# Two rows in place of one: where layer two of an encoder keeps the two parts of its activations

## The chip, the cores and the metric

The kernel runs on one core of a Trainium2 chip. The metric is the device time of one launch in microseconds. It was 2395.79 us, the median of three runs (2395.14 to 2395.84). The profile page and the trace come from one further execution, which took 2398.91 us.

## The reference

Two layers of a bidirectional encoder trunk over 16 learned meta tokens and 256 grid tokens (272 positions, model width 2048). Cut to what matters here:

```python
def _layer(h, w_in, ...):
    proj = einsum('bld,dp->blp', h, w_in)            # 2048 -> 6176 columns
    y_gla = _gla_mixer(gq, gk, gv, gr, glr, ...)     # gated linear attention, 4 heads
    y_na = _na_mixer(nq, nk, nv, na_rel_bias)        # 2-D neighbourhood attention, 16 heads
    mix = einsum('blm,md->bld', concatenate([y_gla, y_na]), w_out)   # 2048 -> 2048
    h = _layer_norm(DEEPNORM_ALPHA * h + mix, ln1_w, ln1_b)
    ff = einsum('blf,fd->bld', square(relu(einsum('bld,df->blf', h, w_ff1))), w_ff2)
    return _layer_norm(DEEPNORM_ALPHA * h + ff, ln2_w, ln2_b)        # 2048 -> 8192 -> 2048
```

The meta tokens are dropped from the output, so the second layer computes many of its products for the 256 grid tokens alone.

## The kernel before

**Activations** lie transposed: a chunk is 128 of the 2048 features on the partitions, positions along the free dimension. There are 16 chunks of `x` (the residual stream, 272 or 256 positions), 16 of `y` (the mixer outputs, later the first half of an MLP hidden half) and 16 of `u` (the other part of the MLP hidden half). Each chunk is kept as two parts, a rounded high part and the remainder, the low part. Both lie in one tile of `ROOM` = 640 floats. Method `pair` opens the tile and `parts` places the two parts in it: the high one `home` floats in, the low one `apart` floats behind the high one. The table `WIDE` gives `(home, apart)`. Layer one uses the first entry. In layer two `x` uses the second while it holds more than 256 columns, and the third, `(36, T)` with T = 256, is used for `y`, `u` and for `x` once the MLP has its normed values: there the two parts touch and make one row of 512 floats.

**Weights** are streamed from memory in tiles of 128 x 1024 floats (512 KB). `made` (from line 138 on) issues the load on the SP queue, ScalarE writes the high part `wh` (line 152) and VectorE the low part `wl` (line 153). Three buffers of each are in rotation. `STARTS` fixes where `wh` and `wl` begin in their buffers for each layer; all of layer two uses the same starts.

**Products.** An exact-enough product is the sum of three: high weight by high part, high weight by low part, low weight by high part. `by_m` walks the output blocks of 128 rows, and for each block the 16 (or, in the second MLP product, 32) input chunks; `three` issues the matmuls of one chunk. With 272, 274 or 258 columns these are three matmuls (lines 165, 166, 167). With exactly 256 columns they are two, here called a pair:

```python
        if n == T:
            mm(ps, lhsT=wh[:, c:c + P], rhs=x.joined, start=first, stop=False)
            mm(ps[:, T:], lhsT=wl[:, c:c + P], rhs=xh[:, :T], start=False, stop=last)
            return
```

The first (line 161) streams both parts, 512 columns, against one load of the high weights; the second (line 162) streams the high part against the low weights. `joined` is an access pattern over both parts: 512 floats in a row where they touch, and two rows of 256 otherwise. `by_k` (line 191) is a second order, used where the input chunks become ready one after another: it takes two chunks at a time for four output blocks and reads the parts separately.

**Order of layer two.** Projections (K, V, q, the output gates, then q, k and v of the neighbourhood attention), in which work of the two attentions is put between the chunks by `pump`; the output projection (first four output blocks by `by_k`, the other twelve by `by_m`); the MLP in two halves, each with eight groups of four output blocks of the first product (inputs `x`) and then 16 blocks of the second product (inputs `y` and `u`). In the first half, groups 0 and 1 use the values before the norm with 258 columns (`fixed`), group 2 is a `by_k` that brings in the normed values through `normed` and `renew`, and all others are pairs. `renew` writes the normed chunk over the old one; in the MLP of layer two it first moves the parts to the third entry of `WIDE`.

Of the kernel before, what the change touches and what calls it, by code (L numbers as in the profile page):

```python
# [17 lines left out]
T = 256  # L18
# [18 lines left out]


ROOM = 640
WIDE = (23, 276), (3, 288), (36, T)  # L40
STARTS = (40, 48), (0, 8)


# [8 lines left out]
class Trunk:  # L52
# [88 lines left out]
    def made(self, ap, parts, l):  # L141
        if ap is None:
            return None
        nc = self.nc
        size = ap.shape[-1]
        raw = self.wp.tile([P, WB], F32, name="raw", tag="raw")[:, :size]
        wh, wl = (self.wp.tile([P, WB + 64], F32R, name=nm, tag=nm)[:, at:at + size]
                  for nm, at in zip(("wh", "wl"), STARTS[l]))
        for p in range(parts):
            c = slice(p * size // parts, (p + 1) * size // parts)  # L150
            nc.sync.dma_start(raw[:, c], ap[:, c])
            nc.scalar.copy(wh[:, c], raw[:, c])  # L152
            self.wl = nc.vector.tensor_tensor(wl[:, c], raw[:, c], wh[:, c].bitcast(F32), ALU.subtract).ins  # L153
        return wh, wl
# [67 lines left out]
    def pair(self, pool, name, c, late=None):  # L222
        if name == "sp":
            return Pair(pool.tile([P, 2, L], F32R, name=f"{name}{c}", tag=f"{name}{c}", bufs=1))
        t = pool.tile([P, ROOM], F32R, name=f"{name}{c}", tag=f"{name}{c}", bufs=1)
        return self.parts(t, *WIDE[(2 if name != "x" else 1) if (self.l if late is None else late) else 0])

    def parts(self, t, home, apart):

        both = t[:, home:home + 2 * apart].rearrange("p (a c) -> p a c", a=2)  # L230
        made = Pair(both)
        made.tile, made.joined = t, t[:, home:home + 2 * T] if apart == T else both[:, :, :T]
        return made


# [635 lines left out]
    def renew(self, end):  # L871

        f = self.norm
        n = f["n"]
        for c in range(f["new"], end):
            while f["ready"] <= c:
                self.step(self.bg, 1)
            if n == T:
                self.x[c] = self.parts(self.x[c].tile, *WIDE[2])
            h, lo = self.x[c]  # L880
            self.split(self.acc[:, c, :n], h[:, :n], lo[:, :n])
        f["new"] = end
# [138 lines left out]
```

## Time and profile before

| | |
|---|---|
| median of three runs | 2395.79 us |
| the profiled execution | 2398.91 us, of which the span is 2396.5 us |
| granted TensorE clock | 0.997 |
| busy: TensorE / VectorE / ScalarE / GpSimd | 2363.8 / 1575.8 / 1187.7 / 284.4 us |
| matmuls | 17276 |
| matmuls of line 161 (512 columns) on x, y, u | 1152, 704, 512 |
| matmuls of line 162 (256 columns) on x, y, u | 1152, 704, 512 |
| read from HBM | 412.57 MB |

Layer two begins at about 1212 us with its K projection. Its projections end at about 1558 us, the output projection at 1652, the MLP's last matmul starts at about 2378 us, and the final norm and the output follow.

How to read it: "busy" of TensorE counts the union of the matmuls' durations, and matmuls overlap, so the pace of a stream is read from the starts in the timeline and not from the busy time. A matmul of 512 columns that takes some 390 to 400 ns starts only some 230 ns ahead of the next.

### The profile page before, as it was taken

The numbers are of one execution on the slowest core, as the hardware profiler recorded it, in microseconds if no ns is written. First come the engines' busy times: TensorE is split into PE (matmuls) and PEld (weight loads), VectorE is DVE, ScalarE is ACT, GpSimd is POOL, SyncE is SP. The second block draws the span as 40 slices with busy tenths as digits, with TensorE's granted clock in tenths as the row PEclk, the third lists the DMA queues.
The fourth block names the chain that finished last, engine by engine and source line by source line (L and its number), as shares of the span: only waits on it lengthen the run. The fifth ranks groups of instructions, "written<-read, shape, count | busy, mean of one in ns | idle before, by whom it ended". The sixth has DMA issues, their size and how long they took to land.

```text
span 2396.5 us, 43078 instructions
## 1 busy us (share of the span) xinstructions
PE 2363.8 (99%) x17276; PEld 2239.3 (93%) x17276; DVE 1575.8 (66%) x2473; ACT 1187.7 (50%) x1962; POOL 284.4 (12%) x447
## 2 busy tenths in 40 slices
PE   9999999999999999999999999999999999999997
PEld 9999999999999999999999898989988888888886
DVE  6688777775544455556577987778765545665655
ACT  6555555564433344444456656555644334444443
POOL 1164320010000000000020653201100000000000
PEclk9999999999999999999999999999999999999998
DMA  7544444555555555555555454455565655565553
GB/s 247 167 142 148 139 147 159 177 182 178 179 182 178 182 177 181 180 178 181 179 178 180 141 153 151 148 166 185 185 188 188 187 185 185 187 188 186 185 188 129
DMA packets 118359, 417.46 MB, mean 174 GB/s; under 512 B 13388, under 2 KB 16332, under 8 KB 118160
## 3 DMA queue, kind: packets, MB, share of 16 engines
q1 hardware_dynamic: 118160, 414.72, 54.6%
q8 instruction: 135, 2.21, 0.4%
q14 instruction: 64, 0.52, 0.1%
HBM read 412.57 MB, written 2.10 MB: 173 GB/s over the span
## 4 chain that ended last, share of the span: by engine, by line
PE 91%; DVE 4%; POOL 2%; issue 1%; ACT 1%; DMA 0%; SPq 0%; ACTq 0%; POOLq 0%; DVEq 0%
PE mm L161 22%; PE mm L165 16%; PE mm L166 16%; PE mm L167 16%; PE mm L162 11%; PE mm L191 5%; POOL lev L475 1%; PE bg L505 1%; DVE wl L153 1%; PE bg L648 1%; DVE acc L864 1%; PE bg L597 0%; ACT ns L580 0%; ACT wh L152 0%; DVE lev L481 0%
## 5 line engine op out<-in xcount | busy, mean ns | idle before, releaser
L153 DVE TENSOR_TENSOR wl<-raw,wh 128x1024 fp32r<-128x1024 f32 (+1 forms) x772 | 945.7, 1226 | 639.1 <-ACT wh L152 630.8
L152 ACT CAST wh<-raw 128x1024 fp32r<-128x1024 f32 (+1 forms) x772 | 804.6, 1043 | 928.2 <-PE mm L166 334.0
L165 PE MATMUL mm<-x,wh 128*128 128x272 f32 (+2 forms) x2176 | 624.3, 287 | 0.0
L166 PE MATMUL mm<-x,wh 128*128 128x272 f32 (+2 forms) x2176 | 617.9, 284 | 0.0
L167 PE MATMUL mm<-x,wl 128*128 128x272 f32 (+2 forms) x2176 | 617.2, 284 | 0.1
L166 PEld LDWEIGHTS mm<-x,wh 128*128 128x128 f32 x2176 | 409.3, 188 | 0.0
L161 PE MATMUL mm<-x,wh 128*128 128x512 f32 x1152 | 409.0, 399 | 0.0
L165 PEld LDWEIGHTS mm<-x,wh 128*128 128x128 f32 x2176 | 407.9, 187 | 1.2 <-issue 0.4
L167 PEld LDWEIGHTS mm<-x,wl 128*128 128x128 f32 x2176 | 407.9, 187 | 0.5 <-DVE wl L153 0.3
L162 PE MATMUL mm<-x,wl 128*128 128x256 f32 x1152 | 323.0, 280 | 0.2 <-DVE wl L153 0.2
L161 PEld LDWEIGHTS mm<-x,wh 128*128 128x128 f32 x1152 | 216.2, 188 | 49.8 <-issue 0.4
L161 PE MATMUL mm<-y,wh 128*128 128x512 f32 x704 | 249.4, 397 | 0.0
L162 PEld LDWEIGHTS mm<-x,wl 128*128 128x128 f32 x1152 | 220.6, 191 | 0.7 <-DVE wl L153 0.6
L166 PE MATMUL mm<-y,wh 128*128 128x272 f32 x704 | 199.2, 283 | 0.0
L165 PE MATMUL mm<-y,wh 128*128 128x272 f32 x704 | 199.2, 283 | 0.0
L167 PE MATMUL mm<-y,wl 128*128 128x272 f32 x704 | 198.9, 283 | 0.0
L162 PE MATMUL mm<-y,wl 128*128 128x256 f32 x704 | 197.2, 281 | 0.7 <-DVE wl L153 0.7
L161 PE MATMUL mm<-u,wh 128*128 128x512 f32 x512 | 181.7, 397 | 0.0
L475 POOL TENSOR_TENSOR lev<-be 128x128 f32<-128x128 f32 (+1 forms) x256 | 150.2, 617 | 112.3 <-PE bg L505 36.3
L161 PEld LDWEIGHTS mm<-y,wh 128*128 128x128 f32 x704 | 132.0, 188 | 30.6 <-ACT wh L152 0.2
L165 PE MATMUL mm<-u,wh 128*128 128x272 f32 x512 | 144.9, 283 | 0.0
L166 PE MATMUL mm<-u,wh 128*128 128x272 f32 x512 | 144.9, 283 | 0.0
(235 smaller groups left out, 3319.4 us busy)
## 6 DMA issues: line engine op xcount, KB each, us to landing
raw<-in_wff SPq DMA_DIRECT2D x512, 512.0 KB, 3.5
raw<-in_win SPq DMA_DIRECT2D x190, 512.0 KB, 3.6
raw<-in_wout SPq DMA_DIRECT2D x64, 512.0 KB, 3.6
nb<-in_nab SPq DMA_DIRECT2D x16, 352.0 KB, 3.9
out<-acc SPq DMA_DIRECT2D x8, 256.0 KB, 2.2
xraw<-in_xT SPq DMA_DIRECT2D x7, 272.0 KB, 5.3
wraw<-in_wup SPq DMA_DIRECT2D x2, 392.0 KB
raw<-in_win SPq DMA_DIRECT2D x4, 128.0 KB, 2.7
```

The lines of the kernel that those rows point to most:

```text
L152: nc.scalar.copy(wh[:, c], raw[:, c])
L153: self.wl = nc.vector.tensor_tensor(wl[:, c], raw[:, c], wh[:, c].bitcast(F32), ALU.subtract).ins
L161: mm(ps, lhsT=wh[:, c:c + P], rhs=x.joined, start=first, stop=False)
L162: mm(ps[:, T:], lhsT=wl[:, c:c + P], rhs=xh[:, :T], start=False, stop=last)
L165: mm(o, lhsT=wh[:, c:c + P], rhs=xh[:, :n], start=first, stop=False)
L166: mm(o, lhsT=wh[:, c:c + P], rhs=xl[:, :n], start=False, stop=False)
L167: mm(o, lhsT=wl[:, c:c + P], rhs=xh[:, :n], start=False, stop=last)
L191: self.nc.tensor.matmul(ps[m][:, :n], lhsT=parts[p][0][:, c:c + P], rhs=acts[j][parts[p][1]][:, :n], start=j + p == 0, stop=j == nk - 1 an ...
L475: tt = lambda o, x, y: nc.gpsimd.tensor_tensor(o, x, y, ALU.subtract)
L505: nc.tensor.matmul(ps[:, b], lhsT=k[:, b], rhs=q[:, r], start=True, stop=True)
L648: nc.tensor.matmul(r[hs], lhsT=(v2 if rest else v1)[:, t, hs], rhs=p2[:, t, :] if rest else p1[:, 2 * t + hh, :], start=rest, stop=not rest)
L864: return self.nc.vector.tensor_tensor(v, v, by[:, None, :].to_broadcast([P, m, n]), alu)
```

## The change

The third entry of `WIDE` goes. Every chunk of layer two, `y` and `u` included, takes the second entry: the high part 3 floats into the tile and the low part 288 floats behind it. `x` stays where it is when `renew` writes the normed values. `joined` is then always the two-row pattern over both parts. The numbers 76 and 204 modulo 256 are the byte addresses of the two rows. No instruction is added or taken away.

```diff
-WIDE = (23, 276), (3, 288), (36, T)
+WIDE = (23, 276), (3, 288)
...
         t = pool.tile([P, ROOM], F32R, name=f"{name}{c}", tag=f"{name}{c}", bufs=1)
-        return self.parts(t, *WIDE[(2 if name != "x" else 1) if (self.l if late is None else late) else 0])
+        return self.parts(t, *WIDE[1 if (self.l if late is None else late) else 0])
 
     def parts(self, t, home, apart):
         both = t[:, home:home + 2 * apart].rearrange("p (a c) -> p a c", a=2)
         made = Pair(both)
-        made.tile, made.joined = t, t[:, home:home + 2 * T] if apart == T else both[:, :, :T]
+        made.joined = both[:, :, :T]
         return made
...
             while f["ready"] <= c:
                 self.step(self.bg, 1)
-            if n == T:
-                self.x[c] = self.parts(self.x[c].tile, *WIDE[2])
             h, lo = self.x[c]
             self.split(self.acc[:, c, :n], h[:, :n], lo[:, :n])
```

## The prediction

> **What bounds the kernel now.** I read the page first: the shares of the engines and the chain that ended last.
>
> ```profile
> span 2396.5 us, 43078 instructions
> PE 2363.8 (99%) x17276; PEld 2239.3 (93%) x17276; DVE 1575.8 (66%) x2473; ACT 1187.7 (50%) x1962; POOL 284.4 (12%) x447
> PE 91%; DVE 4%; POOL 2%; issue 1%; ACT 1%; DMA 0%; SPq 0%; ACTq 0%; POOLq 0%; DVEq 0%
> ```
>
> TensorE is busy for 99% and carries 91% of the chain, so time moves only if TensorE's stream moves. A busy TensorE says nothing of its pace, so next I cut the end of layer two into stretches (columns: length, then busy time and count by engine, granted clock, DMA share, GB/s).
>
> ```profile
> 2016.00:2197.00 181.00, 181.00 (x1026) 158.20 (x1025) 113.16 (x159) 84.98 (x126) 0.00 (x0) 1.00 0.59 186
> 2248.00:2378.00 130.00, 130.00 (x743) 113.15 (x742) 77.87 (x109) 52.75 (x62) 0.00 (x0) 1.00 0.53 170
> 2378.00:2396.50 18.50, 1.15 (x5) 0.59 (x4) 13.24 (x23) 8.32 (x17) 5.70 (x3) 0.58 0.33 113
> ```
>
> In the MLP (the first two rows, TensorE's busy time second) TensorE has no idle time at the full granted clock. What follows its last product is 18.5 us of final norm and output, which the change leaves alone. Whatever the MLP gains comes off the end one for one.
>
> **The pace of a pair.** Where a chunk has 256 columns, line 161 streams high and low part together (512 columns) and line 162 the high part (256): one pair per 128 input rows. Layer two has pairs in both layouts already. The projections read x as two rows (home 3, 288 apart: 12 and 1164 bytes into the tile). The output projection and the MLP read one row (home 36: 144 bytes in). If 12 is 76 modulo 256, a tile starts at 64, the second row lies at 204, and the one row starts at 208. Tiles are 640 floats, ten times 256 bytes, so all of one pool share that residue. The groups by form for four stretches: the q projection, the output projection, a part of that, and the MLP on both sides of 2248 us (count | busy time, mean ns of one | idle before):
>
> ```profile
> L161 PE MATMUL mm<-x,wh 128*128 128x512 f32 x64 | 22.5, 391 | 0.0
> L162 PE MATMUL mm<-x,wl 128*128 128x256 f32 x63 | 17.5, 277 | 0.0
> L161 PE MATMUL mm<-y,wh 128*128 128x512 f32 x192 | 67.5, 397 | 0.0
> L161 PE MATMUL mm<-y,wh 128*128 128x512 f32 x24 | 8.2, 389 | 0.0
> L161 PE MATMUL mm<-x,wh 128*128 128x512 f32 x832 | 294.1, 399 | 0.0
> L162 PE MATMUL mm<-x,wl 128*128 128x256 f32 x832 | 233.8, 281 | 0.0
> L161 PE MATMUL mm<-y,wh 128*128 128x512 f32 x336 | 119.7, 399 | 0.0
> L161 PE MATMUL mm<-u,wh 128*128 128x512 f32 x320 | 114.0, 399 | 0.0
> L161 PE MATMUL mm<-u,wh 128*128 128x512 f32 x192 | 67.7, 395 | 0.0
> L161 PE MATMUL mm<-y,wh 128*128 128x512 f32 x177 | 62.7, 395 | 0.0
> ```
>
> Two rows: 391 and 277 ns (first pair of lines). One row: 397 in the output projection, with a part of it at 389; in the MLP 399 and 281 until about 2248 us, then 395. Products overlap, so the pace has to come from starts. The timeline of TensorE gives the first and last start of unbroken stretches:
>
> ```profile
> 1263.83 0.39 PE L161 MATMUL mm<-x,wh 128*128 128x512 f32 x1
> ...
> 1271.11 0.39 PE L161 MATMUL mm<-x,wh 128*128 128x512 f32 x1
> ...
> 1538.50 0.39 PE L161 MATMUL mm<-x,wh 128*128 128x512 f32 x1
> ...
> 1542.66 0.39 PE L161 MATMUL mm<-x,wh 128*128 128x512 f32 x1
> ...
> 1589.11 0.28 PE L772 MATMUL bg<-sp,onesr 128*128 128x256 f32 x1
> ...
> 1589.68 0.39 PE L161 MATMUL mm<-y,wh 128*128 128x512 f32 x1
> ...
> 1597.16 0.39 PE L161 MATMUL mm<-y,wh 128*128 128x512 f32 x1
> ...
> 1722.14 0.39 PE L161 MATMUL mm<-x,wh 128*128 128x512 f32 x1
> 1722.37 0.28 PE L162 MATMUL mm<-x,wl 128*128 128x256 f32 x1
> 1722.48 0.40 PE L161 MATMUL mm<-x,wh 128*128 128x512 f32 x1
> 1722.72 0.28 PE L162 MATMUL mm<-x,wl 128*128 128x256 f32 x1
> 1722.84 0.40 PE L161 MATMUL mm<-x,wh 128*128 128x512 f32 x1
> ...
> 2016.10 0.40 PE L161 MATMUL mm<-x,wh 128*128 128x512 f32 x1
> ...
> 2197.01 0.40 PE L161 MATMUL mm<-y,wh 128*128 128x512 f32 x1
> ...
> 2248.07 0.28 PE L772 MATMUL bg<-sp,onesr 128*128 128x256 f32 x1
> ...
> 2250.05 0.40 PE L161 MATMUL mm<-u,wh 128*128 128x512 f32 x1
> ...
> 2332.30 0.39 PE L161 MATMUL mm<-y,wh 128*128 128x512 f32 x1
> ```
>
> - Two rows, q projection: 21 pairs in 7.28 us, 346.7 ns a pair.
> - Two rows, last projection: 12 pairs in 4.16 us, 346.7 ns.
> - One row, MLP: 512 pairs in 180.91 us (32 output blocks of 16 chunks), 353.3 ns.
> - One row, after about 2250 us: 235 pairs in 82.25 us, 350.0 ns.
> - One row, a stretch of the output projection: 22 pairs in 7.48 us, 340.0 ns.
>
> So one layout holds three paces at one clock. The stretch at 350.0 begins just after a foreign matmul (the mean of a norm, line 772, at 2248.07) breaks the stream, and so does the one at 340.0 (1589.11): a stream of pairs settles into a rhythm that depends on how it was last broken. The two-row stream is broken every 8 to 24 pairs by attention work, and both stretches quoted, 270 us apart, come back to 346.7.
>
> **The change, part by part.**
>
> 1. *The joined read of line 161 and the 256-column read of line 162.* Pairs affected: output projection 12 products x 16 chunks = 192; the MLP up to the break 832 + 336 + 320 = 1488; after it 192 + 176 = 368 (one of the 177 straddles the cut). Together 2048. I take 346.7 for all of them, since it is the same instruction form with the same weight offsets at the same residues.
>    MLP up to the break: 1488 x (353.3 - 346.7) = 9.8 us. After it: 368 x (350.0 - 346.7) = 1.2 us. The output projection mixes paces: its mean of 397 ns lies a fifth of the way from 399 (pace 353.3) to 389 (pace 340.0), so I estimate 353.3 - 0.2 x 13.3 = 350.6, and 192 x 3.9 = 0.7 us. Sum 11.7 us.
>    Bounds: the best and worst pace that a pair shows here, 340.0 and 353.3. At 340.0: 1488 x 13.3 + 368 x 10.0 + 192 x 10.6 = 19.8 + 3.7 + 2.0 = 25.5 us. At 353.3 everywhere: 368 x 3.3 + 192 x 2.7 = 1.7 us lost. I stay at 346.7, the row nearest in form and place.
>
> 2. *The 384 products of line 191* (third MLP group, and the first of the output projection) read high and low part separately, now at 76 and 204 in place of two places both 208 modulo 256.
>
> ```profile
> 1262.76 0.29 PE L191 MATMUL mm<-x,wh 128*128 128x272 f32 x1
> ...
> 1263.13 0.39 PE L161 MATMUL mm<-x,wh 128*128 128x512 f32 x1
> ...
> 1652.13 0.29 PE L165 MATMUL mm<-x,wh 128*128 128x258 f32 x1
> ...
> 1657.98 0.51 PE L772 MATMUL bg<-sp,onesr 128*128 128x256 f32 x3
> ...
> 1699.49 0.28 PE L191 MATMUL mm<-x,wh 128*128 128x256 f32 x1
> ```
>
>    Now they take (1722.14 - 1699.49) / 192 = 118.0 ns. At the new residues the nearest rows are the last three 272-column products of the group that reads x before the q projection, (1263.13 - 1262.76) / 3 = 123 ns, and the 48 products of 258 columns, (1657.98 - 1652.13) / 48 = 121.9 ns. 256 columns cost 0.24 - 0.12 = 0.12 us by the steps after 1722.48, 0.47 ns a column, so these scale to some 116 and 121 for 256 columns: 384 x (-2 to +3) = -0.8 to +1.2 us. I take 0, as the same line lies on the gaining side and the other on the losing side.
>
> 3. *What writes the chunks* (the split on ScalarE and VectorE at lines 213 and 214) writes the same counts of 256 columns, only elsewhere: no instruction is added or removed. Their cover is the busy TensorE; ScalarE has 96 of 181 us free in the first row of the stretches and VectorE 68.
>
> 4. *The move of x inside its tile* when the normed values replace the raw ones goes away. Its new row overlapped both old ones; now each part lands on its own predecessor. The matmuls waiting on it show no idle time at 1699.49, so 0 either way.
>
> 5. *The weight stream.* A faster TensorE asks for each 512 KB tile every 8 x 346.7 = 2.774 us in place of 2.826. No DMA moves in the program, but this is what would be late next.
>
> ```profile
> SPq L151 <- DVE wl L153: 191.5, 79, 3.7
> q1 hardware_dynamic: 26661, 97.06, 58.8%
> ```
>
>    In the MLP the queue itself waits for VectorE to free a raw buffer (191.5 us in 79 waits) with the rings 58.8% filled, and VectorE in turn is paced by what TensorE has read. At 340.0 (2.72 us a tile) nothing starved for 22 pairs. So nothing.
>
> Sum: 11.7 us. The profiled execution took 2398.91 us (span 2396.5 and 2.4 around it), 3.1 above the median 2395.79; the pairs are the same in both, so I take the saving off the median: 2384.1 us, 0.5% faster.
>
> **The rivals.**
>
> *No change.* The rhythm belongs to the stage and not to the layout: two rows look faster only because attention breaks the stream, and in a stream unbroken for 100 us they too settle at 353.3. Time: 2395.8 + 1.7 at most, some 2396.5. For it: one layout shows three paces. Against: the one row reaches its slow rhythm within a pair or two of 1722.14 (starts 1722.14, 1722.48 and then 353 apart), while two rows hold 346.7 over 21 pairs.
>
> *The good rhythm.* Two rows settle at 340.0 in the MLP. Time 2395.8 - 25.5 = 2370.3. For it: such a rhythm exists. Against: only with one row, and for some 24 pairs of 192.
>
> *Slower: the rows start off a line.* Both 76 and 204 are 12 past a multiple of 16 where 208 is a multiple, so a joined read touches 130 pieces of 16 bytes in place of 128 and line 162 65 in place of 64. If each piece more costs the four columns that it holds, 4 x 0.47 = 1.9 ns, a pair takes 5.6 ns more: 2048 x 5.6 = +11.5 us, 2407.3. It decides if the joined read in the MLP keeps its 399 ns and pays this on top. For it: the 258-column products read 76 and 204 in a long stream at 121.9 ns, above the 118.0 of the reads at 208. Against: the projections' joined read pays no such price, 391 ns against 399.
> The Trainium skill has this rule in "SBUF — State Buffer", Specifications: SBUF lines are 16 bytes and each crossing to a new one pays a penalty. By that rule alone the change could only lose; this trace's 391 against 399 disagrees.
>
> **How the numbers follow.** A measurement of this kernel tells 0.2%, 4.8 us, from no change. Pace 346.7 or near it in nearly all of the stream: 0.76, 2382 to 2387. A mixture of 346.7 with stretches at 350 and above: 0.06, 2387 to 2392. The good rhythm: 0.05, 2370. No change: 0.07. Slower: 0.06. Faster is 0.76 + 0.05 + 0.05 of the mixtures (those under 2391.0) = 0.86; same 0.07 + 0.01 = 0.08; slower 0.06. The range takes in the likeliest case, its unknown of -0.8 to +1.2 us, the mixtures, and half of the way to the good rhythm: 2377 to 2392, leaving out some 0.18.
>
> **What the profile after would show.** Right: line 161 with x, y and u in the MLP at 391 ns and line 162 at 277; 512 pairs of the second half's first product in 177.5 us in place of 180.9; the busy TensorE shorter by 12 us; the queue still waiting for VectorE. Step 2 right: line 191 at 280 to 282 ns. Wrong: 399 in the MLP (the stage sets the rhythm), or 391 with waits of line 161 or 162 on VectorE or ScalarE at the weights (the stream of weights is next), or a pace above 353.

## The result, and the profile after

The kernel after took 2386.38 us (median, 2386.06 to 2386.67) against 2395.67 for the kernel before, six runs each: a ratio of 0.9961, 95% interval 0.9948 to 0.9974. Timed again in a later round it took 2386.69 us, at 0.9949 (0.9936 to 0.9961) of the kernel before. It was forecast at 2384.1; the gain was 9.3 us where 11.7 were forecast.

The page of the kernel after: span, busy times, and the chain that ended last.

```profile
span 2384.2 us, 43078 instructions
PE 2351.7 (99%) x17276; PEld 2230.9 (94%) x17276; DVE 1576.1 (66%) x2473; ACT 1187.5 (50%) x1962; POOL 283.5 (12%) x447
PE 92%; DVE 4%; POOL 2%; issue 1%; ACT 1%; DMA 0%; SPq 0%; ACTq 0%; POOLq 0%; DVEq 0%
```

The instructions are the same in number, TensorE is 12.1 us less busy with its matmuls (PE) and 8.4 us less with its weight loads (PEld), and the span is 12.3 us shorter; no other engine moved by a microsecond. The groups by form of the kernel after (count | busy time, mean ns of one | idle before): the output projection, the MLP up to the foreign matmul near its end, and the rest.

```profile
L161 PE MATMUL mm<-y,wh 128*128 128x512 f32 x192 | 66.6, 391 | 0.0
...
L161 PE MATMUL mm<-x,wh 128*128 128x512 f32 x832 | 288.5, 391 | 0.0
L162 PE MATMUL mm<-x,wl 128*128 128x256 f32 x832 | 231.0, 278 | 0.0
L161 PE MATMUL mm<-y,wh 128*128 128x512 f32 x336 | 117.5, 391 | 0.0
...
L161 PE MATMUL mm<-u,wh 128*128 128x512 f32 x192 | 67.1, 390 | 0.0
L161 PE MATMUL mm<-y,wh 128*128 128x512 f32 x176 | 61.7, 390 | 0.0
```

The 399 ns are gone everywhere. The line of the 832 pairs on x holds the pace too: each product of line 161 outlasts the step to the next pair, so the busy time of an unbroken group is its stretch, and 288.5 / 832 = 346.8 ns (before, 294.1 / 832 = 353.5). This is 0.1 to 0.2 ns above the step from starts, as the last product of each stretch counts in full. Most experiments below are read by this line. The timeline of TensorE shows the pace directly, and the borders of the stages:

```profile
1583.28 0.39 PE L161 MATMUL mm<-y,wh 128*128 128x512 f32 x1
...
1651.20 0.28 PE L165 MATMUL mm<-x,wh 128*128 128x258 f32 x1
...
1698.50 0.28 PE L191 MATMUL mm<-x,wh 128*128 128x256 f32 x1
...
1720.87 0.39 PE L161 MATMUL mm<-x,wh 128*128 128x512 f32 x1
...
2009.30 0.39 PE L161 MATMUL mm<-x,wh 128*128 128x512 f32 x1
...
2186.79 0.39 PE L161 MATMUL mm<-y,wh 128*128 128x512 f32 x1
...
2236.92 0.28 PE L772 MATMUL bg<-sp,onesr 128*128 128x256 f32 x1
...
2237.51 0.39 PE L161 MATMUL mm<-u,wh 128*128 128x512 f32 x1
...
2320.36 0.39 PE L161 MATMUL mm<-y,wh 128*128 128x512 f32 x1
...
2365.17 0.39 PE L161 MATMUL mm<-u,wh 128*128 128x512 f32 x1
```

512 pairs of the second half's first product take 177.49 us, 346.7 ns each. Over all 2048 pairs, line 162 starts 230 ns behind line 161 where it was 237, and the next pair 117 ns behind line 162 where it was 116: the gain lies behind the 512-column product. After the foreign matmul of 2236.92, where the kernel before had changed to 350.0, 239 pairs take 82.85 us, 346.7 ns again. Two more rows of the kernel before, its first and last pair of the stages in question, complete the comparison:

```profile
1583.28 0.39 PE L161 MATMUL mm<-y,wh 128*128 128x512 f32 x1
...
2377.49 0.40 PE L161 MATMUL mm<-u,wh 128*128 128x512 f32 x1
```

Output projection, pairs: 68.85 to 67.92 us, 0.9 gained. MLP, first to last pair: 655.35 to 644.30, 11.05 gained. Third MLP group (line 191): 22.65 to 22.37, 0.3 gained. That is the whole of the 12.3 us between the profiles but for 0.05.

The SP queue's own waits up to the foreign matmul, and the stretch that answers to the first one shown of before:

```profile
SPq L151 <- DVE wl L153: 187.4, 79, 3.7
2009.00:2187.00 178.00, 178.00 (x1028) 155.92 (x1028) 113.17 (x159) 85.07 (x127) 0.00 (x0) 1.00 0.61 190
```

The queue still waits for VectorE, and TensorE never for weights.

### The profile page after: what moved, and what is told of

Read it like the earlier page. It is cut to its first block, busy times and chain, and to the rows that moved or that the text cites. A ratio compares the mean times of both kernels' runs of the same rounds, so it can differ in the third digit from the quotient of the medians.

```text
span 2384.2 us, 43078 instructions
## 1 busy us (share of the span) xinstructions
PE 2351.7 (99%) x17276; PEld 2230.9 (94%) x17276; DVE 1576.1 (66%) x2473; ACT 1187.5 (50%) x1962; POOL 283.5 (12%) x447
## 4 chain that ended last, share of the span: by engine, by line
PE 92%; DVE 4%; POOL 2%; issue 1%; ACT 1%; DMA 0%; SPq 0%; ACTq 0%; POOLq 0%; DVEq 0%
PE mm L161 22%; PE mm L165 16%; PE mm L166 16%; PE mm L167 16%; PE mm L162 11%; PE mm L191 6%; POOL lev L475 1%; PE bg L505 1%; DVE wl L153 1%; PE bg L648 1%; DVE acc L864 1%; PE bg L597 1%; ACT wh L152 0%; ACT ns L580 0%; DVE lev L481 0%
## 5 line engine op out<-in xcount | busy, mean ns | idle before, releaser
L161 PE MATMUL mm<-x,wh 128*128 128x512 f32 x1152 | 403.5, 393 | 0.0
```

## The experiments

**Is the gap between a profiled execution and the median the profile's doing?** The kernel before, with the tile width written another way:

```diff
-ROOM = 640
+ROOM = 10 * 64
```

> The kernel before, unchanged but for how the tile width is written (10 * 64 for 640). Asked: why its profiled execution took 2398.9 us where its other runs take 2395.7, while the kernel after shows no such gap. Theory A (the one-row stream has several rhythms and each execution falls into them differently): times 2395 to 2396.5 us, and this profile shows another split of the MLP's 1856 pairs between 353.3 and 350.0 ns or better, with a profiled time that differs from 2398.9 by 3.3 ns per pair that changed sides. Theory B (the profile itself costs this kernel 3 us): the same split to within 20 pairs and again 2398 to 2399.5 us in the profiled execution.

Measured: 2399.71 us (2398.75 to 2400.6 in ten runs), ratio 1.0 (0.9991 to 1.001); its profiled execution took 2400.23. The kernel before itself took 2395.42 to 2395.70 in three runs there and 2398.15 to 2400.71 in 22. The trace of this execution, timeline near the end, up to the last pair ahead of the next break:

```profile
2248.33 0.28 PE L772 MATMUL bg<-sp,onesr 128*128 128x256 f32 x1
...
2249.97 0.39 PE L161 MATMUL mm<-u,wh 128*128 128x512 f32 x1
...
2330.53 0.39 PE L161 MATMUL mm<-u,wh 128*128 128x512 f32 x1
...
2370.11 0.40 PE L161 MATMUL mm<-y,wh 128*128 128x512 f32 x1
```

After the same foreign matmul 228 pairs take 80.56 us, 353.3 ns, where the first execution had 350.0. It lasts to the next break, for some 345 pairs: 345 x 3.3 = 1.1 of the 1.3 us between the two profiled times. So executions of one program do fall into different rhythms, as theory A says, though its times were wrong: no run of this copy was under 2398.75. Theory B falls, as the other runs took as long as the profiled one. A second repetition was meant to catch the quick group:

> The kernel before once more, for its rhythm in another execution on another chip. Theory A (its executions fall into different rhythms): if the profiled time is near 2395.5, more pairs at 340.0 or 350.0 than the two profiles at hand, some 3 us in all, that is 300 pairs 10 ns or 900 pairs 3.3 ns faster; if it is near 2399, the split of those two again.

Measured: 2399.13 us in eight runs (2398.48 to 2400.5), ratio 1.0002 (0.9992 to 1.0012); profiled at 2398.48, with x at 353.5 ns as in the other two:

```profile
L161 PE MATMUL mm<-x,wh 128*128 128x512 f32 x832 | 294.1, 399 | 0.0
```

No profile shows the quick group of 2394.8 to 2396.4 us. Its share differs from round to round (6 of 6 runs of the kernel before beside the result, then 3 of 25, 13 of 19 and 1 of 15). Where its 3 us lie, and what decides between the groups, stays open.

**Two rows, or the place of the row?** Three layouts of `y`, `u` and the normed `x`; the projections keep theirs. One row, started at 76:

```diff
-WIDE = (23, 276), (3, 288), (36, T)
+WIDE = (23, 276), (3, 288), (3, T)
```

> One row as before, moved so that it starts at 76 modulo 256 (home 3 in place of 36). Position theory (it is the place of the first byte that sets the rhythm): pairs at 346.7 ns, 2386 us. Distance theory (what counts is that high and low row lie 128 apart modulo 256) and form theory (what counts is that the read is broken into two rows): one row keeps several rhythms at 350 to 353 ns, 2394 to 2398 us.

Two rows at 208 and 80 (third entry `(36, 288)`, `joined` as in the kernel after):

```diff
-WIDE = (23, 276), (3, 288), (36, T)
+WIDE = (23, 276), (3, 288), (36, 288)
-        made.tile, made.joined = t, t[:, home:home + 2 * T] if apart == T else both[:, :, :T]
+        made.tile, made.joined = t, both[:, :, :T]
```

> Two rows for y, u and the normed x, but at 208 and 80 modulo 256 (home 36, 288 apart): the distance of after with the start of before. Distance theory and form theory: 346 to 347 ns a pair, 2386 us. Position theory (first byte at 208 is the bad place): 350 to 353 ns, 2394 to 2398 us.

Two rows both at 208 (320 floats apart; the third entry is `(36, 320)`, and `joined` is as above):

```diff
...
+        if apart == 320:
+            both = t.rearrange("p (a c) -> p a c", a=2)[:, :, home:]
...
```

> Two rows at 208 and 208 modulo 256 (home 36, 320 apart): every read starts at the residue that it has in the kernel before, only that the row is broken between the parts. Form theory: 346 to 347 ns a pair, 2386 us. Distance theory and position theory: 350 to 353 ns and more than one rhythm, 2394 to 2398 us.

The x group of the three, in this order:

```profile
L161 PE MATMUL mm<-x,wh 128*128 128x512 f32 x832 | 288.5, 391 | 0.0
```
```profile
L161 PE MATMUL mm<-x,wh 128*128 128x512 f32 x832 | 291.3, 394 | 0.0
```
```profile
L161 PE MATMUL mm<-x,wh 128*128 128x512 f32 x832 | 294.1, 399 | 0.0
```

One row at 76: 346.8 ns, 2386.75 us, ratio 0.9948 (0.9933 to 0.9963). Two rows at 208 and 80: 350.1 ns, 2393.38 us, 0.9977 (0.9968 to 0.9987). Two rows at 208 and 208: 353.5 ns, 2399.52 us, 1.0001 (0.9992 to 1.0011). Breaking the row does nothing by itself, so the form theory falls. A row at 76 gets the whole gain unbroken, so the distance theory falls as well: the place makes the pace. It is not the place of the first byte alone, as the position theory had it: the last two layouts both begin at 208, and the second row at 80 in place of 208 is worth 3.4 ns a pair.

**Place within 256 bytes, or within 16?** One row a float to either side, `(4, T)` and `(35, T)` for `(36, T)`:

```diff
-WIDE = (23, 276), (3, 288), (36, T)
+WIDE = (23, 276), (3, 288), (4, T)
```

> One row starting at 80 modulo 256 (home 4), one float behind the fast row at 76. Theory P (the place within 256 bytes, against the weights at 64 and 96, makes the rhythm): four bytes change little, 346.7 ns a pair, 2386 to 2388 us. Theory M (what counts is the start modulo 16: 12 is fast and 0 slow): 350 to 353 ns with several rhythms, 2394 to 2400 us.

> One row starting at 204 modulo 256 (home 35), one float ahead of the slow row at 208. Theory P (place within 256): still slow, 350 to 353 ns, 2394 to 2400 us. Theory M (start modulo 16): 346.7 ns, 2386 to 2388 us.

```profile
L161 PE MATMUL mm<-x,wh 128*128 128x512 f32 x832 | 286.7, 389 | 0.0
```
```profile
L161 PE MATMUL mm<-x,wh 128*128 128x512 f32 x832 | 288.5, 389 | 0.0
```

The ratios at 80 and 204, with the weights alone moved, and for half of the change are taken against runs with a median of 2395.47, from the quick group; the other ratios of this section against 2399.18 or 2398.7, from the slower one. So layouts are compared by their ns. At 80: 344.6 ns, 2382.59 us, ratio 0.9944 (0.9929 to 0.9959). At 204: 346.8 ns, 2386.91 us, 0.9963 (0.9949 to 0.9977). Four bytes make 6.7 ns a pair between 204 and 208 and 2.2 the other way between 76 and 80. Neither theory held: P missed 204, and M missed 80, a multiple of 16 and the quickest of all.

**The weights' place.** The kernel before with layer two's weights moved:

```diff
-STARTS = (40, 48), (0, 8)
+STARTS = (40, 48), (33, 41)
```

> The kernel before with layer two's weights moved by 33 floats (starts 33 and 41 in place of 0 and 8), so that the row at 208 lies as far behind the high weights, modulo 256, as the fast row at 76 lay (12 bytes). All of layer two is touched, the 272-column products and the projections' pairs too, so only the MLP's pairs are read. Theory R (what counts is the moving row's place against the weights'): MLP pairs at 346.7 ns, MLP and output projection together 11 us shorter than before. Theory M or P (the moving row's own start): MLP pairs at 350 to 353 ns.

And with the row moved along, `(37, T)` for `(36, T)`:

> Weights moved by 33 floats as before (starts 33 and 41) and the one row moved by 33 floats against the good one at 80 (home 37, 212 modulo 256), so that row and weights stand to each other as in the kernel with one row at 80. Only the MLP's pairs are read. Theory R (only the distance between moving row and weights counts, modulo 256): the MLP's pairs repeat 344.4 ns, in the same cycle of three pairs. Theory W (both starts count, each for itself): another pace than 344.4, with the weights-moved kernel's 346.7 the nearest.

```profile
L161 PE MATMUL mm<-x,wh 128*128 128x512 f32 x832 | 288.5, 394 | 0.0
```
```profile
L161 PE MATMUL mm<-x,wh 128*128 128x512 f32 x832 | 299.6, 399 | 0.0
```

With the weights alone moved, the row at 208 that ran at 353.5 runs at 346.8 (2390.47 us, ratio 0.9975, 0.9965 to 0.9985; its MLP is as short as after; the 272-column products of the projections are slower, line 166 from 123.5 to 127.4 ns between starts). So the weights' start is part of the rhythm. Not for every row: the q projection's pairs, at 76 and 204, keep some 347 ns with the moved weights (23 pairs in 7.97 us, first and last here).

```profile
1263.65 0.39 PE L161 MATMUL mm<-x,wh 128*128 128x512 f32 x1
...
1271.62 0.39 PE L161 MATMUL mm<-x,wh 128*128 128x512 f32 x1
```

Moved together, row and weights stand to each other as in the quickest layout, and the pace is the slowest seen: 360.1 ns, 2416.8 us, 1.0076 (1.006 to 1.0091). Theory R falls; both starts count. That it would be slower than any other layout, theory W did not say.

**Half of the change.** `x` stays in two rows; `y` and `u` keep the one row:

```diff
-            if n == T:
-                self.x[c] = self.parts(self.x[c].tile, *WIDE[2])
```

> Half of the change: x stays in two rows at 76 and 204, while y and u keep the one row at 208. If each pair's pace goes by where its own chunk lies: the 832 pairs on x at 346.7, the 1216 on y and u at 350 to 353, a gain of 832 x 6.6 = 5.5 us, 2390 to 2394 us. If one slow kind of chunk in the stream holds the rhythm for the others: x pairs also near 353 and no gain.

```profile
L161 PE MATMUL mm<-x,wh 128*128 128x512 f32 x832 | 288.5, 391 | 0.0
L161 PE MATMUL mm<-y,wh 128*128 128x512 f32 x332 | 117.1, 395 | 0.0
...
1832.55 0.40 PE L161 MATMUL mm<-y,wh 128*128 128x512 f32 x1
...
2011.76 0.39 PE L161 MATMUL mm<-x,wh 128*128 128x512 f32 x1
...
2189.25 0.40 PE L161 MATMUL mm<-y,wh 128*128 128x512 f32 x1
```

2390.38 us, ratio 0.9973 (0.9964 to 0.9983). The x group is 5.6 us shorter, as counted for 832 pairs. By the timeline 512 pairs on x take 177.49 us, 346.7 ns, right behind 512 pairs on y and u, still in the old place, that take 179.21 us, 350.0 ns. So x has the pace of its own place beside chunks that lie elsewhere. For y and u the place leaves several rhythms open: in this stage every profile of the kernel before has them at 353.3. What set them to 350.0 here, one profile cannot tell. One of the ten runs took 2386.52, a jump of 3.9 us like that to the quick group, and not profiled either.

**The quicker place beside the change.** Both again, on one chip:

> The kernel after, unchanged, timed beside the one row at 80 and the kernel before on one chip. One rhythm in all its executions (346.7 ns a pair): 2386 to 2387 us, spread under 1.5 us.

> One row at 80 modulo 256 (home 4), timed beside the kernel after. If its 344.4 ns a pair is a property of the place and not of a lucky execution: 2382 to 2384 us in every run and 3.5 to 4.5 us under the kernel after. If it was luck: runs at 2386 and above among them.

The kernel after: 2386.69 us (2385.79 to 2386.81). One row at 80: 2383.12 us, 2382.73 to 2383.36 in four runs, ratio 0.9934 (0.9921 to 0.9948) against the kernel before. Its profiled execution took 7394 us and is left out. The lead is 3.6 us: 2048 pairs x 2.2 = 4.5, less what the 384 products of line 191 lose at this place, 0.65 us in the trace of its first round. One row at 80 beats both kernels.

## Why the prediction was right, point by point

- **What bounds it.** Right: TensorE's stream alone moved, and the end moved with it.
- **Step 1, the pairs.** 346.7 ns was taken from the projections and 346.7 was measured, in 512 pairs without a break as in the broken stream. MLP 11.05 us against 9.8 + 1.2; output projection 0.9 against 0.7. The grounds given were "the same instruction form with the same weight offsets at the same residues". Of these the form was idle: two rows at 208 and 208 ran as slowly as one. It was the residues. The weights' start moves the pace of the old row (353.5 to 346.8), but the q projection's pairs at 76 and 204 showed no such step when the weights moved.
- **Step 2, line 191.** Taken at 0 in a range of -0.8 to +1.2 us; the third MLP group gained 0.3 (116.5 ns a product in place of 118.0). The scaled 272-column rows, not the 258-column ones, were the right neighbour. The sign that it named, a mean of 280 to 282 ns, did not come: it was 280 and 281 before and is 278 and 277 after.
- **Steps 3 to 5.** Right: VectorE and ScalarE are as busy as before, the MLP's products of line 191 show no idle time in either trace, and the queue's wait for VectorE went from 191.5 to 187.4 us. One reading was off: the 58.8% of the line on queue q1 is the share of the 16 DMA engines' time that its packets took, not how far rings are filled. Nothing in the sum hung on it.
- **The sum.** Here lies the miss of 2.3 us. Between the two profiled executions the gain is 12.5 us (2398.91 to 2386.44), within a microsecond of the sum. The step that failed is "the pairs are the same in both, so I take the saving off the median". They were not the same: executions of the kernel before lie either at 2394.8 to 2396.4 or at 2397.9 to 2400.7, the profiled one in the slower group and the median in the quicker. The kernel after has no second group. 2398.91 - 11.7 = 2387.2 would have been nearer.
- **"No change".** Wrong as a mechanism: the two-row stream held its pace over 1484 unbroken pairs.
- **"The good rhythm".** It did not come with 76 and 204; at 80 a quicker one (344.4) held over 1484 unbroken pairs and 345 more, though not in the last 17 (346.4).
- **"Slower: the rows start off a line".** 204 is quicker than 208 by 6.7 ns, off a 16-byte line quicker than on it; 80 is quicker than 76 by 2.2, on the line quicker than off. The Trainium skill's rule in "SBUF — State Buffer", Specifications, that each crossing to a new 16-byte line pays a penalty, gives the second order and not the first; the measurement decides.

## What to carry to other kernels

When TensorE is 99% busy, read the step from start to start in two stages that differ in layout: here a few nanoseconds a pair showed there, and in the mean ns of one product, while the busy share stayed at 99%, and the pace measured in one stage carried over to another exactly. Moving an operand's start by a few bytes is a change worth measuring, for the streamed operand and for the weights together, since neither fixed the pace alone. And check whether the profiled execution lies in the middle of the runs before a sum made against it is taken off their median.

## What the runs showed of the hardware

The step of one and the same pair of matmuls (512 and 256 columns, full clock, no wait) ran from 344.6 to 360.1 ns, as a mean over 832 pairs, by where the streamed row and the weights begin:

| streamed rows (high, low), modulo 256 | weights (high, low) | ns a pair, 832 on x |
|---|---|---|
| 80, one row | 64, 96 | 344.6 |
| 76, one row | 64, 96 | 346.8 |
| 76 and 204, two rows | 64, 96 | 346.8 |
| 204, one row | 64, 96 | 346.8 |
| 208 and 80, two rows | 64, 96 | 350.1 |
| 208, one row | 64, 96 | 353.5 |
| 208 and 208, two rows | 64, 96 | 353.5 |
| 208, one row | 196, 228 | 346.8 |
| 212, one row | 196, 228 | 360.1 |

(The places of the weights take their tile's start at 64, like that of the activations; no run shows either start.) 80 and 208 lie 128 bytes apart and differ by 8.9 ns, so more than the place within 128 bytes counts; that it repeats after 256 was not tried. At 208 against 64 and 96 the stream has several rhythms, 340.0, 350.0 and 353.3, and in the profiles of the kernel before it kept the one that a break left it in until the next break; at 76 and 204 every unbroken stretch of 12 pairs or more came back to 346.6 to 347.1. The Trainium skill, "TensorE: Matmul & The Clock Gate", Step-by-step, gives TensorE two independent read ports, by which loading the next weights takes no read bandwidth from the running matmul; here moving the weights alone changed the step from 353.5 to 346.8 ns, and whether the ports have a part in that no run shows. What rule ties the two starts to the pace is not settled by these runs.
